# An explicit order for the opening, later pieces of w_out, and a forward SSD pass that carries its state ahead and gates a chunk behind

## The chip, the cores and the metric

The kernel runs on one core of a Trainium2 chip. The core has a matrix engine (PE), a vector engine (DVE), an activation engine (ACT) and a general engine (POOL), which issues DMAs too; SP only issues DMAs. Every engine works through its own instructions in the order in which they were laid out, and waits on semaphores of the others. The metric is the device time of one execution in microseconds (us). It was 908.02 us, the median of three runs (901.15 to 909.67).

## The reference, cut to what matters

One encoder layer on x (1024 positions, 1024 channels). A root-mean-square norm and one projection feed two groups of heads: a Mamba-2 SSD in both directions, in chunks of 128 positions, for two groups of 8 heads; and windowed attention. Each has a gate, their outputs meet in the product with w_out, and the residual and a last norm follow.

```
h = rms_norm(x, norm_in_g);  proj = h @ w_in
z, xbc, dt_raw, q, k, v, ga = split(proj);  xbc = silu(conv(xbc) + conv_b)
# SSD, per direction, chunk c:
scores = (C_c B_c^T) * exp(cs_l - cs_s)        # masked, per head
y_c    = scores @ X_c + (C_c S_c) * exp(cs_l)  # y_diag + y_off
S_c+1  = decay_c * S_c + B_c^T (decay * X_c)   # state, carried
y = y_fwd + y_bwd + d_skip * xs
y_ssd  = rms_norm_per_group(y * silu(z))
y_attn = rms_norm(windowed_gqa(q, k, v) * silu(ga))
out = rms_norm(x + concat(y_ssd, y_attn) @ w_out) * final_g
```

## The kernel before, in words

**Matrix products.** The large products split each float32 operand into a high and a low part (`hi`, `lo`) and add three products. One block of w_in (128 output channels) is 8 slices by 3 products, 24 matmuls of 512 positions for each half of the positions: `proj_steps`, line 146 before and 154 after. They are called projections below.

**Opening.** Eight tiles of x (128 positions each) are loaded, normed on ACT or DVE with POOL's power (lines 212 to 218), transposed by PE against the identity (220) and split into `hhi` on ACT and `hlo` on DVE (224, 225), in four quarters of 256 positions. Two blocks of w_in run along with the quarters.

**SSD.** For g = 0, 1: a backward pass over chunks 7 to 0, then a forward pass over 0 to 7. In the backward pass `y_off` (PE, line 570, then DVE 572) adds its part into `yb_d` in device memory by an accumulating DMA from POOL (579), and `advance` carries the state: POOL makes `xd` (542), ACT and DVE split it into `xh`, `xl` (545, 546), PE multiplies (552), POOL decays the old state (557) and DVE adds (558). In the forward pass `scores` makes M of a chunk: 8 ACT rows on E (607), a DVE addition on F (608), DVE minimum (609), ACT scaling and exponent (612, 613), three DVE products. The chunk's `yb` is y_off, to which POOL's accumulating DMA (630) adds `yb_d`; DVE adds the product with M (635, 637); POOL gates with z (`yg`, 643), ACT squares (646), POOL folds the squares (647, 649) and SP stores.

**Order.** `fill(n)` takes n halves of the projections that are still to be done. Where an instruction ends up on its engine is decided by a scheduler at build time, which estimates durations; the program's text gives only the order in which the work is named. With `tc.issue_after(x)` the text binds an instruction behind x.

**w_out.** 32 pieces (`chore`: load, two ACT copies, a POOL difference) are split during attention; `chores_up_to(32)` takes those that are left before the last products.

Of the kernel before, what the change touches and what calls it, by code (L numbers as in the profile page):

```python
# [16 lines left out]
P = 128  # L17
# [18 lines left out]
def kernel(  # L36
# [74 lines left out]
    def load_parameters():  # L111
        nc.sync.dma_start(out=prm_sb, in_=prm)
        V.tensor_scalar(out=cw, in0=cw, scalar1=0.5, scalar2=None, op0=ALU.mult)

    def rsqrt(dst, src, scale, eps):
        n = src.shape[1]
        V.tensor_scalar(out=dst, in0=src, scalar1=scale, scalar2=eps, op0=ALU.mult, op1=ALU.add)
        G.tensor_tensor(out=dst, in0=dst, in1=nhalf[:, 0:n], op=ALU.pow)
# [64 lines left out]
    both = rows(s1.tile([P, NH], F32, name="sink2"), sink, NH), rows(s1.tile([P, NH], F32, name="dsk2"), d_skip, NH)  # L183
    dtb = rows(s1.tile([P, 32], F32, name="dtb"), dt_bias, 32)
    Ab = rows(s1.tile([P, 32], F32, name="Ab"), a_log, 32)
    rb = s1.tile([64, NH], F32, name="rb")
    G.memset(rb, NEG)
    G.dma_start(out=rb[0:32], in_=rel_bias)

    dsk = gp.tile([P, NH // 2], F32, name="dsk")  # L190
    msk = gp.tile([P, 2, P], F32, name="msk")
    G.dma_start(out=msk, in_=c_tri)
    xts = [cp.tile([P, S + 4], F32, tag="pad", name="xt0")[:, 0:D]]
    xts += [tiles[3][:, 2 * i:2 * i + 2, :].rearrange("p b e -> p (b e)") for i in range(4)]
    xts += [cp.tile([P, S + 4], F32, tag="pad", name="xt5")[:, 0:D], tiles[1], tiles[0]]
    for sb, xt in enumerate(xts):
        nc.sync.dma_start(out=xt, in_=x[sb * P:(sb + 1) * P, :])
        if sb == 0:
            load_parameters()
        if sb in (1, 2):  # L200
            blk = XBC0 + 6 + 2 * sb
            pre[blk] = load_split(w_blk[blk], [P, NKB, P], wp, eng=V)
    whi, wlo = load_split(w_vdt, [P, NKB, 288], s1, tag="wv", eng=G)
    for q in range(4):
        sh, o = divmod(q, 2)
        cols = slice(o * 256, o * 256 + 256)
        banks = [bank(t) for t in ("mm t s y", "t s t s", "t s t s", "t s y t")[q].split()]
        for j, xt in enumerate(xts[2 * q:2 * q + 2]):
            junk = cp.tile([P, D], F32, tag="acc", name="junk")
            ss = s1.tile([P, 1], F32, tag="ss", name="ss", bufs=8)  # L210
            if q == j == 0:
                V.tensor_tensor_reduce(out=junk, in0=xt, in1=xt, scale=1.0, scalar=0.0, op0=ALU.mult,
                                       op1=ALU.add, accum_out=ss)
            else:
                A.activation(out=junk, in_=xt, func=AF.Square, accum_out=ss)
            rs = s1.tile([P, 1], F32, tag="rs", name="rs", bufs=8)
            rsqrt(rs, ss, 1.0 / D, EPS)
            V.tensor_scalar(out=xt, in0=xt, scalar1=rs, scalar2=None, op0=ALU.mult)
            for kb in range(NKB):
                T.transpose(banks[kb // 2][:, (kb % 2) * 256 + j * P:(kb % 2) * 256 + (j + 1) * P],  # L220
                            xt[:, kb * P:(kb + 1) * P], ident)
        for kb in range(NKB):
            ps = banks[kb // 2][:, (kb % 2) * 256:(kb % 2) * 256 + 256]
            A.activation(out=hhi[sh][:, kb, cols], in_=ps, func=AF.Copy, scale=g_in[:, kb:kb + 1])  # L224
            V.scalar_tensor_tensor(out=hlo[sh][:, kb, cols], in0=ps, scalar=g_in[:, kb:kb + 1],
                                   in1=hhi[sh][:, kb, cols].bitcast(F32),
                                   op0=ALU.mult, op1=ALU.subtract)
        for blk, ws in pre.items():
            if o == 0:
                early.setdefault(blk, []).append(bank("mm"))  # L230
            for _ in proj_steps(early[blk][sh][:, cols], ws, sh, cols):
                pass
# [248 lines left out]
    def v3(t):  # L481
        return t.rearrange("p (h d) -> p h d", h=HPG)
# [40 lines left out]
    for g in range(NG):  # L523
# [15 lines left out]

        def weighted(c, d):  # L540
            xd = sp.tile([P, 512], F32, tag="xd", name="xd")
            G.tensor_tensor(out=v3(xd), in0=v3(xk[:, c, :]), in1=bc(hb(wst, d, c, g), 64), op=ALU.mult)
            xh = sp.tile([P, 512], F32R, tag="xh", name="xh", bufs=1)
            xl = sp.tile([P, 512], F32R, tag="xl", name="xl", bufs=1)
# [4 lines left out]
        def advance(Sold, c, d):  # L549
            ps = bank("s")  # L550
            for i, (b, x) in enumerate(zip((Bk[0], Bk[0], Bk[1]), weighted(c, d))):
                T.matmul(ps, lhsT=b[:, c, :], rhs=x, start=i == 0, stop=i == 2)
            Sn = sp.tile([P, 512], F32, tag="S", name=f"S{d}")
            if Sold is None:
                A.activation(out=Sn, in_=ps, func=AF.Copy)
            else:
                G.tensor_tensor(out=v3(Sn), in0=v3(Sold), in1=bc(hb(dec, d, c, g), 64), op=ALU.mult)
                V.tensor_tensor(out=Sn, in0=Sn, in1=ps, op=ALU.add)
            return Sn
# [27 lines left out]
        def scores(c):  # L587
# [10 lines left out]
            CB = sp.tile([P, 2, P], F32, tag="CB", name="CB")  # L598
# [9 lines left out]
            V.tensor_tensor(out=F, in0=F, in1=bc(hb(ncs, 1, c, g), P), op=ALU.add)  # L608
# [11 lines left out]
        Mn = scores(0)  # L620
        for c in range(NSB):
            M = Mn
            if c < NSB - 1:
                Mn = scores(c + 1)
            yb = sp.tile([P, 512], F32, tag="yo", name="yb", bufs=3)
            if Sf is None:
                nc.sync.dma_start(out=yb, in_=yb_d[g, c])
            else:
# [11 lines left out]
            zt = sp.tile([P, 4, P], F32, tag="zt", name="zt", bufs=1)  # L640
            nc.sync.dma_start(out=zt, in_=z_d[g * 4:(g + 1) * 4, :, c * P:(c + 1) * P].rearrange("b p s -> p b s"))
            yg = sp.tile([P, 512], F32, tag="yg", name="yg", bufs=1)
            G.tensor_tensor(out=yg, in0=yb, in1=zt.rearrange("p b s -> p (b s)"), op=ALU.mult)
            nc.sync.dma_start(out=y_d[g, c], in_=yg)
            y2 = sp.tile([P, 512], F32, tag="y2", name="y2", bufs=1)
            A.activation(out=y2, in_=yg, func=AF.Square)
            G.tensor_tensor(out=y2[:, 0:256], in0=y2[:, 0:256], in1=y2[:, 256:512], op=ALU.add)
            sqs = sp.tile([P, P], F32, tag="sqs", name="sqs", bufs=6)
            G.tensor_tensor(out=sqs, in0=y2[:, 0:P], in1=y2[:, P:256], op=ALU.add)
            sums.append((g, c, sqs))  # L650
# [26 lines left out]
    def outputs():  # L677
# [51 lines left out]
        chores_up_to(32)  # L729
        for sb in range(NSB):  # L730
# [19 lines left out]
            for part in range(2):  # L750
                ys.append(parts(load_y(o_d[sb, part])))
                for dh, c0, c1 in cuts if sb < NSB - 1 else []:
                    yield from products(pss[dh], ys[part], range(8 + 4 * part, 12 + 4 * part), dh,
                                        part == 0, part == 1)
# [306 lines left out]
```

## Time and profile before

| | before |
|---|---|
| median of three runs | 908.02 us |
| the profiled execution | 900.58 us, span 898.8 us |
| PE busy | 848.2 us (94%) |
| DVE busy | 569.2 us (63%) |
| ACT busy | 491.3 us (55%) |
| POOL busy | 356.6 us (40%) |

Busy shares are means over the whole span: an engine with 40% can still be the one that is waited for in a stage of its own. Three stages are named below by their times: the opening (0 to 50 us), the backward pass of g = 1 (386.6 to 443.1 us) and its forward pass with what follows until attention starts (443.1 to 542.1 us).

### The profile page before, as it was taken

The page shows a single profiled execution, that of the slowest core. Times are in us where ns is not written, and L with a number is a line of the kernel's source. Part 1 is how long each engine was busy: PE and PEld are TensorE (multiplying, and loading weights), DVE is VectorE, ACT ScalarE, POOL GpSimd, SP SyncE. Part 2 cuts the span into 40 slices and gives each one's busy share as a digit, 9 for nine tenths or more (in the row PEclk, how much of TensorE's full clock was granted, in tenths as well). Part 3 has the DMA queues.
Part 4 walks back from the last instruction along what each step waited for, and adds up shares of the span by engine and source line. Part 5 has one row for each costly group of instructions (what it writes and reads, how often), then busy time and mean ns, then how long its engine had stood idle before and what let it go on. Part 6 is the DMA issues. An engine that isn't in the chain of part 4 may idle for free. (4 is left out here: it accounts for less than half of the span.)

```text
span 898.8 us, 13352 instructions
## 1 busy us (share of the span) xinstructions
PE 848.2 (94%) x4622; PEld 714.6 (80%) x4622; DVE 569.2 (63%) x971; ACT 491.3 (55%) x1118; POOL 356.6 (40%) x327
## 2 busy tenths in 40 slices
PE   3999999998898999999979999999999999899997
PEld 2999788886677888888857787887888888688786
DVE  4575766596898375446769945655766767555433
ACT  4642474353656345523645725788867866764222
POOL 3300012533865201134358552273653741735622
PEclk9999999999999999999998999999999999999999
DMA  8122473576788513477859869869856757424421
GB/s 296 75 83 59 155 222 128 141 222 187 223 234 256 166 47 94 117 206 177 261 131 253 225 190 246 243 200 308 245 149 182 221 131 190 145 56 136 132 87 47
DMA packets 127408, 154.25 MB, mean 172 GB/s; under 512 B 42331, under 2 KB 79899, under 8 KB 127212
## 3 DMA queue, kind: packets, MB, share of 16 engines
q1 hardware_dynamic: 121420, 141.35, 51.4%
q0 software_dynamic: 5776, 11.79, 7.4%
q8 instruction: 36, 0.59, 0.3%
q14 instruction: 32, 0.26, 0.1%
q10 hardware_dynamic: 144, 0.26, 0.1%
HBM read 111.58 MB, written 43.88 MB: 173 GB/s over the span
## 5 line engine op out<-in xcount | busy, mean ns | idle before, releaser
L146 PE MATMUL mm<-hhi,whi 128*128 128x512 f32 (+1 forms) x640 | 247.2, 389 | 1.8 <-ACT hhi L224 1.8
L146 PE MATMUL mm<-hlo,whi 128*128 128x512 f32 (+1 forms) x640 | 246.9, 387 | 0.0
L146 PE MATMUL mm<-hhi,wlo 128*128 128x512 f32 (+1 forms) x640 | 246.5, 386 | 0.0
L146 PEld LDWEIGHTS mm<-hhi,whi 128*128 128x128 f32 x640 | 121.6, 191 | 23.5 <-ACT hhi L224 2.5
L146 PEld LDWEIGHTS mm<-hlo,whi 128*128 128x128 f32 x640 | 121.9, 191 | 22.5 <-issue 1.7
L146 PEld LDWEIGHTS mm<-hhi,wlo 128*128 128x128 f32 x640 | 121.9, 191 | 21.7 <-issue 0.7
L695 PE MATMUL mm<-hhi,yl 128*128 128x512 f32 (+1 forms) x264 | 104.8, 397 | 0.8 <-POOL yl L687 0.8
L695 PE MATMUL mm<-hhi,yh 128*128 128x512 f32 (+1 forms) x264 | 104.7, 397 | 0.0
L695 PE MATMUL mm<-hlo,yh 128*128 128x512 f32 (+1 forms) x264 | 104.6, 396 | 0.0
L880 DVE CUSTOM_DVE_ANT_0 lg<-s,bias,nsnk 128x320 f32<-128x320 f32 (+2 forms) x128 | 64.6, 521 | 43.5 <-PE s L877 42.6
L883 ACT ACTIVATE lg<-lg,nm 128x320 f32<-128x320 f32 (+2 forms) x128 | 68.5, 535 | 18.3 <-DVE nm L880 16.4
L250 DVE SCALAR_TENSOR_TENSOR acc<-pad,prm_sb,acc 128x1024 f32<-128x1024 f32 x48 | 62.1, 1301 | 24.4 <-ACT acc L247 23.1
L687 POOL TENSOR_TENSOR yl<-y,yh 128x512 fp32r<-128x512 f32 x32 | 41.8, 1306 | 82.6 <-ACT yh L686 63.8
L134 ACT ACTIVATE whi<-wraw 128x1024 fp32r<-128x1024 f32 x38 | 40.0, 1054 | 41.9 <-PE mm L146 38.1
L137 POOL TENSOR_TENSOR wlo<-wraw,whi 128x1024 fp32r<-128x1024 f32 x12 | 30.2, 2518 | 69.0 <-ACT whi L134 69.0
L695 PEld LDWEIGHTS mm<-hhi,yl 128*128 128x128 f32 x264 | 50.2, 190 | 7.0 <-POOL yl L687 1.2
L607 ACT ACTIVATE cb<-cb,ncs 128x128 f32<-128x128 f32 x128 | 39.4, 390 | 29.8 <-DMA cb<-cs_d 29.8
L695 PEld LDWEIGHTS mm<-hhi,yh 128*128 128x128 f32 x264 | 50.3, 190 | 5.6
L695 PEld LDWEIGHTS mm<-hlo,yh 128*128 128x128 f32 x264 | 50.1, 190 | 5.5
L897 DVE TENSOR_TENSOR pl<-t,ph 128x512 fp32r<-128x512 f32 (+1 forms) x64 | 40.6, 654 | 18.7 <-ACT ph L896 18.0
L435 POOL TENSOR_TENSOR hlo<-oraw,hhi 128x512 fp32r<-128x512 f32 x32 | 41.0, 1292 | 26.6 <-ACT hhi L434 24.7
L137 DVE TENSOR_TENSOR wlo<-wraw,whi 128x1024 fp32r<-128x1024 f32 x26 | 33.7, 1297 | 24.0 <-ACT whi L134 21.4
(233 smaller groups left out, 1749.8 us busy)
## 6 DMA issues: line engine op xcount, KB each, us to landing
wraw<-in_w_blk_dram SPq DMA_DIRECT2D x38, 512.0 KB, 4.2
cb<-cs_d SPq DMA_DIRECT2D x32, 512.0 KB, 5.8
qt<-q_d SPq DMA_DIRECT2D x32, 256.0 KB, 3.8
oraw<-in_w_out_dram SPq DMA_DIRECT2D x32, 256.0 KB, 4.0
et<-es_d SPq DMA_DIRECT2D x56, 128.0 KB, 4.9
yb_d<-pad SPq DMA_DIRECT2D x8, 512.0 KB, 3.9
z_d<-gz SPq DMA_DIRECT2D x16, 256.0 KB, 3.8
zt<-z_d SPq DMA_DIRECT2D x16, 256.0 KB, 3.7
```

Of the source, the lines that this page charges most:

```text
L134: A.activation(out=hi, in_=raw, func=AF.Copy)
L137: eng.tensor_tensor(out=lo, in0=raw, in1=hi.bitcast(F32), op=ALU.subtract)
L146: yield T.matmul(ps, lhsT=l[:, kb, :], rhs=r[sh][:, kb, cols], start=(n == 0), stop=(n == 3 * NKB - 1))
L250: V.scalar_tensor_tensor(out=acc, in0=pad[:, k:k + S], scalar=cw[:, blk * 6 + k:blk * 6 + k + 1], in1=acc, op0=ALU.mult, op1=ALU.add)
L435: G.tensor_tensor(out=lo[:, c:c + 512], in0=raw, in1=hi[:, c:c + 512].bitcast(F32), op=ALU.subtract)
L607: A.activation(out=E[:, h, :], in_=E[:, h, :], func=AF.Identity, bias=ncs[:, 0, c, hh:hh + 1])
L687: G.tensor_tensor(out=lo, in0=t, in1=hi.bitcast(F32), op=ALU.subtract)
L695: yield T.matmul(ps[:, cols], lhsT=l[:, j * P:(j + 1) * P], rhs=r[:, dh * 512 + cols.start:dh * 512 + cols.stop], start=first and n == 0, ...
L880: V.tensor_tensor_reduce(out=l, in0=ps[:, d0 - c0:d1 - c0], in1=bias[:, hp, d0 - f0:d1 - f0], scale=-1.0, scalar=nsnk[:, sk], op0=ALU.add, ...
L883: A.activation(out=l, in_=l, func=AF.Exp, scale=-1.0, bias=nm, accum_out=sm)
L897: V.tensor_tensor(out=pl[0:w, 0:n], in0=ps[0:w, 0:n], in1=ph[0:w, 0:n].bitcast(F32), op=ALU.subtract)
```

## The change

1. **Opening.** `in_line` binds each instruction behind the one before on its engine, so norms, transposes, splits and the two early blocks stand in the order of the text. The parameters are loaded after the second x tile, the two early weight blocks after the second and fourth (they came after the second and third), and the small tables, loaded by POOL, go behind the last of POOL's norms.
2. **w_out.** The pieces are split just before the product that needs them, or one behind every third matmul of the first block; the call for all 32 is gone.
3. **Forward SSD.** The state goes ahead of the chunk's product with M, and `xd`, `xh`, `xl` of the next chunk are made ahead. The product with M is added first, and then POOL's DMA adds `yb_d`. Gating (`finish`) and folding (`reduce`) come one chunk later, and y is stored from ACT's queue. The masked CB stays in PSUM. The addition on F is now 8 ACT rows instead of one DVE instruction. `ordered` ties POOL's instructions of the SSD, its DMAs included, to one sequence, in the backward pass too.

```diff
+        def ordered(trace):
+            with ExitStack() as st:
+                if last[0] is not None:
+                    st.enter_context(tc.issue_after(last[0].ins))
+                last[0] = trace()
...
-                G.dma_start(out=yb_d[g, c], in_=yo, accum_op=ALU.add)
+                ordered(lambda: G.dma_start(out=yb_d[g, c], in_=yo, accum_op=ALU.add))
...
-            CB = sp.tile([P, 2, P], F32, tag="CB", name="CB")
+            CB = ps[:, P:3 * P].rearrange("p (d l) -> p d l", d=2)
...
-            V.tensor_tensor(out=F, in0=F, in1=bc(hb(ncs, 1, c, g), P), op=ALU.add)
+                A.activation(out=F[:, h, :], in_=F[:, h, :], func=AF.Identity, bias=ncs[:, 1, c, hh:hh + 1])
...
-        Mn = scores(0)
+        Mn, xw, ready = scores(0), weighted(0, 0), None
         for c in range(NSB):
             M = Mn
             if c < NSB - 1:
                 Mn = scores(c + 1)
             yb = sp.tile([P, 512], F32, tag="yo", name="yb", bufs=3)
-            if Sf is None:
-                nc.sync.dma_start(out=yb, in_=yb_d[g, c])
-            else:
+            first = Sf is None
+            if not first:
                 y_off(Sf, c, 0, yb)
-                G.dma_start(out=yb, in_=yb_d[g, c], accum_op=ALU.add)
+            if c < NSB - 1:
+                Sf = advance(Sf, c, 0, xw)
+            y2 = finish(*ready) if ready else None
+            if c < NSB - 2:
+                xw = weighted(c + 1, 0)
+            if y2 is not None:
+                reduce(c - 1, y2)
             fill(FORWARD[c][0])
...
-            V.tensor_tensor(out=yb, in0=py, in1=yb, op=ALU.add)
-            if c < NSB - 1:
-                Sf = advance(Sf, c, 0)
...
+            if first:
+                V.tensor_copy(yb, py)
+            else:
+                V.tensor_tensor(out=yb, in0=py, in1=yb, op=ALU.add)
+            ordered(lambda: G.dma_start(out=yb, in_=yb_d[g, c], accum_op=ALU.add))
+            ready = c, yb
...
+        reduce(NSB - 1, finish(*ready))
...
+                chores_up_to(2 * kb + 2)
...
-        chores_up_to(32)
```

PE in the forward pass of g = 1, before, from the product with the state of chunk 1 (`CT,S`; `xh`, `xl` are the operands of `advance`, `M,xk` the product with M, `mm` the projections):

```order
L570 MATMUL s<-CT,S_3950 128x128 x4
L552 MATMUL s<-xh,Bk_2737 128x512
L552 MATMUL s<-xl,Bk_2737 128x512
L552 MATMUL s<-xh,Bk_2738 128x512
L146 MATMUL mm<-hhi_100,wlo 128x512
L146 MATMUL mm<-hhi_100,whi 128x512
L146 MATMUL mm<-hlo_102,whi 128x512
```

The same place now, from the last product of the backward pass to the third of the forward pass:

```order
L154 MATMUL mm<-hhi_99,wlo 128x512
L627 MATMUL s<-CT,S_3633 128x128 x4
L713 MATMUL y<-M,xk 64x128 x8
L611 MATMUL s<-xh,Bk_2785 128x512
L611 MATMUL s<-xl,Bk_2785 128x512
L611 MATMUL s<-xh,Bk_2786 128x512
L653 MATMUL t<-CT,BT 128x128
L627 MATMUL s<-CT,S_3812 128x128 x4
```

No projection follows here until attention's first product; before, 11 to 48 stood in a chunk. Counted from the first `advance` of the group, the backward pass now holds 444 projections (193 before) and the forward pass none (266 before until attention).

POOL in the forward pass of g = 1, before:

```order
L643 TENSOR_TENSOR yg<-yb,zt 128x512
L630 DMA yb<-yb_d 128x512
L137 TENSOR_TENSOR wlo<-wraw,whi 128x1024
L557 TENSOR_TENSOR S_4198<-S_4056,dec 128x512
L647 TENSOR_TENSOR y_3958<-y_3958 128x256
L542 TENSOR_TENSOR xd<-xk,wst 128x512
```

and now, one chunk and the next DMA:

```order
L719 DMA yb<-yb_d 128x512
L608 TENSOR_TENSOR S_4103<-S_3955,dec 128x512
L681 TENSOR_TENSOR yg<-yb,zt 128x512
L598 TENSOR_TENSOR xd<-xk,wst 128x512
L688 TENSOR_TENSOR y_4114<-y_4114 128x256
L690 TENSOR_TENSOR sqs<-y_4114 128x128
L719 DMA yb<-yb_d 128x512
```

The gating of a chunk (`yg`) now stands behind its own DMA and ahead of the next chunk's DMA; before, the next DMA was issued straight behind `yg` and landed beside the work after it.

## Rows read from the trace of the kernel before

**Rows 1.** PE and the rest by stage: us, busy (x instructions), granted PE clock.

```profile
0.00:20.00 20.00, 6.18 (x25) 5.12 (x26) 7.34 (x16) 8.36 (x14) 7.61 (x26) 1.00 0.86 283
...
386.60:443.10 56.50, 56.50 (x285) 46.89 (x284) 37.71 (x46) 25.13 (x61) 22.79 (x19) 1.00 0.79 202
443.10:528.80 85.70, 75.64 (x418) 60.73 (x416) 66.77 (x77) 44.26 (x107) 51.84 (x41) 0.96 0.75 207
528.80:542.10 13.30, 13.25 (x73) 10.79 (x73) 3.81 (x6) 2.66 (x4) 6.99 (x10) 1.00 0.58 175
...
205.70:289.30 83.60, 74.19 (x427) 59.18 (x425) 68.84 (x76) 46.65 (x115) 51.74 (x41) 0.98 0.77 230
```

**Rows 2.** What PE waited for, whole span: us in total, times, longest.

```profile
PE mm L220 <- DVE xt L218: 11.9, 1, 11.9
PE y L635 <- DVE yb L637: 6.2, 3, 2.4
PE s L552 <- DVE xl L546: 5.7, 5, 2.2
...
PE t L891 <- DVE pl L897: 3.4, 1, 3.4
```

**Rows 3.** Two projections in PE's timeline, 17 starts apart (start, us).

```profile
389.37 0.39 PE L146 MATMUL mm<-hhi,whi 128*128 128x512 f32 x1
...
393.22 0.40 PE L146 MATMUL mm<-hhi,wlo 128*128 128x512 f32 x1
```

**Rows 4.** DMA issues: KB each, median us to landing; then line 630's minimum, median, maximum.

```profile
yb_d<-yo POOLq DMA_DIRECT2D x14, 256.0 KB, 5.4
yb<-yb_d POOLq DMA_DIRECT2D x14, 256.0 KB, 5.7
...
DMA to landing us min/median/max: 4.1/5.7/6.8
```

**Rows 5.** Groups of POOL instructions: busy, mean ns | idle before, releaser.

```profile
L542 POOL TENSOR_TENSOR xd<-xk,wst 128x512 f32<-128x512 f32 x28 | 31.5, 1129 | 20.8 <-DVE xl L546 17.5 <-ACT xk L265 3.3
L643 POOL TENSOR_TENSOR yg<-yb,zt 128x512 f32<-128x512 f32 x16 | 26.9, 1680 | 38.7 <-DVE yb L637 35.3 <-DMA zt<-z_d 3.2
L647 POOL TENSOR_TENSOR y<-y 128x256 f32<-128x256 f32 x16 | 19.3, 1207 | 6.1 <-ACT y L646 6.1
L649 POOL TENSOR_TENSOR sqs<-y 128x128 f32<-128x128 f32 x16 | 12.1, 755 | 0.8
```

**Rows 6.** Groups of the scores and the state, on ACT and DVE.

```profile
L607 ACT ACTIVATE cb<-cb,ncs 128x128 f32<-128x128 f32 x128 | 39.4, 390 | 29.8 <-DMA cb<-cs_d 29.8
L612 ACT ACTIVATE M<-CB,dt 128x128 f32<-128x128 f32 x128 | 38.9, 390 | 0.8 <-DVE CB L600 0.7
L608 DVE TENSOR_TENSOR cb<-cb,ncs 128x1024 f32<-128x1024 f32 x16 | 22.2, 1386 | 13.2 <-DMA cb<-cs_d 13.2
L613 ACT ACTIVATE cb<-cb 128x1024 f32<-128x1024 f32 x16 | 16.9, 1057 | 18.9 <-DVE cb L609 18.8
```

**Rows 7.** POOL in the forward pass of g = 1 (timeline).

```profile
463.21 0.72 POOL L647 TENSOR_TENSOR y<-y 128x256 f32<-128x256 f32 x1 [0.74 <-ACT y L646]
...
470.77 1.27 POOL L643 TENSOR_TENSOR yg<-yb,zt 128x512 f32<-128x512 f32 x1 [3.52 <-DVE yb L637]
471.99 0.90 POOL L630 DMA_DIRECT2D yb<-yb_d  x1
...
480.70 0.45 POOL L649 TENSOR_TENSOR sqs<-y 128x128 f32<-128x128 f32 x1
```

**Rows 8.** The opening: three rows of the timeline, then a group.

```profile
4.25 1.22 DVE L212 CUSTOM_DVE_ANT_0 junk<-xt 128x1024 f32<-128x1024 f32 x1 [4.25 <-DMA xt<-in_x_dram]
...
11.09 0.74 DVE L218 TENSOR_SCALAR xt<-xt,rs 128x1024 f32<-128x1024 f32 x1
...
50.28 0.30 PE L286 MATMUL mm<-wvhi,hhi 128*128 128x288 f32 x1
...
L225 DVE SCALAR_TENSOR_TENSOR hlo<-t,prm_sb,hhi 128x256 fp32r<-128x256 f32 x14 | 6.7, 480 | 7.4 <-ACT hhi L224 7.2
```

More of the change, by code (lines that the diff above doesn't have):

```diff
@@ L112, in load_parameters @@
         nc.sync.dma_start(out=prm_sb, in_=prm)
-        V.tensor_scalar(out=cw, in0=cw, scalar1=0.5, scalar2=None, op0=ALU.mult)
     def rsqrt(dst, src, scale, eps):
@@ L117, in rsqrt, with in_line @@
         V.tensor_scalar(out=dst, in0=src, scalar1=scale, scalar2=eps, op0=ALU.mult, op1=ALU.add)
-        G.tensor_tensor(out=dst, in0=dst, in1=nhalf[:, 0:n], op=ALU.pow)
+        return G.tensor_tensor(out=dst, in0=dst, in1=nhalf[:, 0:n], op=ALU.pow)
+    def in_line(line, trace):
+        with ExitStack() as st:
+            for ins in line.values():
+                st.enter_context(tc.issue_after(ins.ins))
+            ins = trace()
+        line[str(ins.ins.engine)] = ins
+        return ins
     pa = ctx.enter_context(ExitStack())
@@ L181, in rows, with small_tables @@
         return t
[L183 to L192, printed above, removed]
+    def small_tables():
+        both = rows(s1.tile([P, NH], F32, name="sink2"), sink, NH), rows(s1.tile([P, NH], F32, name="dsk2"), d_skip, NH)
+        dtb = rows(s1.tile([P, 32], F32, name="dtb"), dt_bias, 32)
+        Ab = rows(s1.tile([P, 32], F32, name="Ab"), a_log, 32)
+        rb = s1.tile([64, NH], F32, name="rb")
+        G.memset(rb, NEG)
+        G.dma_start(out=rb[0:32], in_=rel_bias)
+        dsk = gp.tile([P, NH // 2], F32, name="dsk")
+        msk = gp.tile([P, 2, P], F32, name="msk")
+        G.dma_start(out=msk, in_=c_tri)
+        return both, dtb, Ab, rb, dsk, msk
     xts = [cp.tile([P, S + 4], F32, tag="pad", name="xt0")[:, 0:D]]
@@ L195 @@
     xts += [cp.tile([P, S + 4], F32, tag="pad", name="xt5")[:, 0:D], tiles[1], tiles[0]]
+    raw = {}
     for sb, xt in enumerate(xts):
         nc.sync.dma_start(out=xt, in_=x[sb * P:(sb + 1) * P, :])
-        if sb == 0:
+        if sb == 1:
             load_parameters()
[L200 to L203, printed above, removed]
+        if sb in (1, 3):
+            blk = XBC0 + 7 + sb
+            raw[blk] = wp.tile([P, NKB, P], F32, tag="wraw", name="wraw", bufs=3)
+            nc.sync.dma_start(out=raw[blk], in_=w_blk[blk])
@@ new lines, with split_first, norm @@
+    line = {}
+    def split_first(blk):
+        hi = wp.tile([P, NKB, P], F32R, tag="whi", name="whi")
+        lo = wp.tile([P, NKB, P], F32R, tag="wlo", name="wlo")
+        in_line(line, lambda: A.activation(out=hi, in_=raw[blk], func=AF.Copy))
+        in_line(line, lambda: V.tensor_tensor(out=lo, in0=raw[blk], in1=hi.bitcast(F32), op=ALU.subtract))
+        pre[blk] = hi, lo
+    def norm(i):
+        xt = xts[i]
+        junk = cp.tile([P, D], F32, tag="acc", name="junk")
+        ss = s1.tile([P, 1], F32, tag="ss", name="ss", bufs=8)
+        if i in (0, 4):
+            in_line(line, lambda: V.tensor_tensor_reduce(out=junk, in0=xt, in1=xt, scale=1.0, scalar=0.0,
+                                                         op0=ALU.mult, op1=ALU.add, accum_out=ss))
+        else:
+            in_line(line, lambda: A.activation(out=junk, in_=xt, func=AF.Square, accum_out=ss))
+        rs = s1.tile([P, 1], F32, tag="rs", name="rs", bufs=8)
+        in_line(line, lambda: V.tensor_scalar(out=rs, in0=ss, scalar1=1.0 / D, scalar2=EPS, op0=ALU.mult, op1=ALU.add))
+        in_line(line, lambda: G.tensor_tensor(out=rs, in0=rs, in1=nhalf[:, 0:1], op=ALU.pow))
+        in_line(line, lambda: V.tensor_scalar(out=xt, in0=xt, scalar1=rs, scalar2=None, op0=ALU.mult))
@@ new lines, with turn @@
+    tbanks = {}
+    def turn(i):
+        q, j = divmod(i, 2)
+        if j == 0:
+            tbanks[q] = [bank(t) for t in ("mm t s y", "t s t s", "t s t s", "t s y t")[q].split()]
+        for kb in range(NKB):
+            o = (kb % 2) * 256 + j * P
+            in_line(line, lambda: T.transpose(tbanks[q][kb // 2][:, o:o + P], xts[i][:, kb * P:(kb + 1) * P], ident))
+    norm(0)
+    norm(1)
+    V.tensor_scalar(out=cw, in0=cw, scalar1=0.5, scalar2=None, op0=ALU.mult)
+    turn(0)
+    turn(1)
@@ L204 @@
+    first, second = raw
+    split_first(first)
     for q in range(4):
@@ L206 @@
         cols = slice(o * 256, o * 256 + 256)
[L207 to L213, printed above, removed]
-            else:
[L215 to L221, printed above, removed]
-        for kb in range(NKB):
[L223 to L227, printed above, removed]
+        for kb in range(NKB):
+            ps = tbanks[q][kb // 2][:, (kb % 2) * 256:(kb % 2) * 256 + 256]
+            g, h, l = g_in[:, kb:kb + 1], hhi[sh][:, kb, cols], hlo[sh][:, kb, cols]
+            in_line(line, lambda: A.activation(out=h, in_=ps, func=AF.Copy, scale=g))
+            in_line(line, lambda: V.scalar_tensor_tensor(out=l, in0=ps, scalar=g, in1=h.bitcast(F32),
+                                                         op0=ALU.mult, op1=ALU.subtract))
+            if kb % 4 == 3 and q < 3:
+                norm(2 * q + 2 + kb // 4)
+        if q == 0:
+            split_first(second)
         for blk, ws in pre.items():
@@ L230 @@
                 early.setdefault(blk, []).append(bank("mm"))
-            for _ in proj_steps(early[blk][sh][:, cols], ws, sh, cols):
-                pass
+            steps = proj_steps(early[blk][sh][:, cols], ws, sh, cols)
+            for n in range(3 * NKB):
+                in_line(line, lambda: next(steps))
+                if blk == second and q < 3 and n in (0, 12):
+                    turn(2 * q + 2 + n // 12)
+    whi, wlo = load_split(w_vdt, [P, NKB, 288], s1, tag="wv", eng=G)
+    with tc.issue_after(line["EngineType.Pool"].ins):
+        both, dtb, Ab, rb, dsk, msk = small_tables()
     for t, src in zip((snk, dsk), both):
@@ L538 @@
             kv_pools.append(pool(ctx, "kvp", side="left"))
+        last = [None]
+        def ordered(trace):
+            with ExitStack() as st:
+                if last[0] is not None:
+                    st.enter_context(tc.issue_after(last[0].ins))
+                last[0] = trace()
         def weighted(c, d):
[L541 to L544, printed above, removed]
+            xd = sp.tile([P, 512], F32, tag="xd", name="xd", bufs=1)
+            ordered(lambda: G.tensor_tensor(out=v3(xd), in0=v3(xk[:, c, :]), in1=bc(hb(wst, d, c, g), 64), op=ALU.mult))
+            xh = sp.tile([P, 512], F32R, tag="xh", name="xh")
+            xl = sp.tile([P, 512], F32R, tag="xl", name="xl")
             A.activation(out=xh, in_=xd, func=AF.Copy)
@@ L547, in weighted, with advance @@
             return xh, xl, xh
-        def advance(Sold, c, d):
+        def advance(Sold, c, d, xw=None):
+            Sn = sp.tile([P, 512], F32, tag="S", name=f"S{d}")
+            if Sold is not None:
+                ordered(lambda: G.tensor_tensor(out=v3(Sn), in0=v3(Sold), in1=bc(hb(dec, d, c, g), 64), op=ALU.mult))
             ps = bank("s")
-            for i, (b, x) in enumerate(zip((Bk[0], Bk[0], Bk[1]), weighted(c, d))):
+            for i, (b, x) in enumerate(zip((Bk[0], Bk[0], Bk[1]), xw or weighted(c, d))):
                 T.matmul(ps, lhsT=b[:, c, :], rhs=x, start=i == 0, stop=i == 2)
-            Sn = sp.tile([P, 512], F32, tag="S", name=f"S{d}")
             if Sold is None:
@@ L752, in outputs @@
                 for dh, c0, c1 in cuts if sb < NSB - 1 else []:
-                    yield from products(pss[dh], ys[part], range(8 + 4 * part, 12 + 4 * part), dh,
-                                        part == 0, part == 1)
+                    for n, m in enumerate(products(pss[dh], ys[part], range(8 + 4 * part, 12 + 4 * part), dh,
+                                                   part == 0, part == 1)):
+                        yield m
+                        if sb == part == 0 and n % 3 == 2:
+                            chore()
             for i, (dh, c0, c1) in enumerate(cuts):
```

28 lines of the change are left out of this document (15 added, 13 removed).

## The prediction, made before the changed kernel ran

> **What bounds the kernel now.** I read the busy shares first: PE works 94% of the span, so a change pays only where PE stands, and costs wherever it makes PE stand. The windows by stage show where that is. The opening leaves PE busy for 6.2 of 20 us. In g = 1 the backward pass (386.6 to 443.1 us) has PE busy through all of its 56.5 us; the forward pass and its tail (443.1 to 528.8) leave 10.1 us of 85.7 open, and the last 13.3 us before attention are full. The forward pass of g = 0 leaves 9.4 us open [rows 1]. The list of PE's waits names the causes: 11.9 us for the first normed tile, and in the SSD, at most 2.4 us at a time, 6.2 us for DVE's yb and 5.7 for its xl [rows 2]. So all that a better forward pass can win is the open part of the two stages, about 20 us, with at most 14 us in the opening; behind that is the matmul work itself.
>
> **What fills PE in the SSD.** The chain of the state is thin for PE: a chunk of the forward pass needs some 2.5 us of it. The rest are projections, one every 0.2265 us (3.85 us for 17 starts [rows 3]). Whoever spends projections early has none later. This is what the new order does: 444 stand in the backward pass of g = 1 instead of 193, and none in the forward pass. The count comes from the order, the price from the rows.
>
> **Backward pass of g = 1.** 251 projections more, at 0.2265 us, are 57 us, and PE had no idle time there to take them in [rows 1]; the pass grows from 56.5 to about 113.5 us. Tying POOL's instructions into a sequence costs nothing here: between a y_off and the `advance` behind it stand 40 to 46 projections, 9 to 10.5 us, while the six steps between (y_off's DVE row, POOL's DMA issue of 0.90 [rows 7], decay, xd of 1.13 [rows 5], the splits on ACT and DVE), none of them longer than yg's 1.68, come to at most 8.8 us. If that cover were gone, PE would stand up to 8.8 us per chunk.
>
> **Forward pass of g = 1.** With nothing to fill it, its length is that of its slowest engine's sequence. POOL's is now a closed ring per chunk: issue the DMA that adds yb_d, wait until it has landed (the decay lies within), gate (`yg`), make `xd` of the chunk after next, fold, fold again, issue the next DMA. `yg` cannot pass its own DMA and the next DMA cannot pass the folds. The landing is 5.7 us in the median, between 4.1 and 6.8 [rows 4]; yg 1.68, xd 1.13, the folds 1.21 and 0.755 [rows 5]: 10.5 us a chunk. Before, the DMA of the next chunk was issued straight behind yg, 471.99 after the yg of 470.77, and its flight lay beside the folds, xd and decay [rows 7]. Six chunks with xd at 10.5 and two without at 9.35 make 81.7 us. The ring can start only when the backward pass's last addition to yb_d has landed (5.4 us [rows 4], with a product and a DVE row ahead of it: I take 7 us after the last product). Sum: 88 us; I take 86, since the first products with M stand ready and the last wait overlaps attention's first rows. All of this replaces 85.7 + 13.3 = 99.0 us [rows 1], and 15 projections (3.4 us) are left for attention: 57 + 86 + 3.4 − 99 = **+47 us**. PE has about 20 us of work in these 86.
>
> The bounds: with the shortest landing [rows 4] and the shortest yg and folds (1.27, 0.72, 0.45 [rows 7]) a chunk takes 7.7 us and the pass 66, which gives +27. From above, ACT's work per chunk is not much shorter than the ring: L607 costs 39.4/16 = 2.46 us a chunk, and now twice (F moves over from DVE, which saves it 1.39 us there [rows 6]), L612 2.43, the exponent 1.06 [rows 6]: 8.4 us, without the copies for the state and the squares. Where both sequences wait for one another, 12.5 us a chunk are possible, 107 us in all: +68. I stay with 10.5, since the ring's members have the more direct rows.
>
> A rule stands against the landing time. The Trainium skill, "DMA: Bandwidth & Descriptors", section "Anatomy of one DMA — SWDGE (gpsimd) path", gives a fit of 2.0 us plus the bytes at 436 GB/s for a DMA from this engine, 2.6 us for 256 KB by my estimate from it; then a chunk would take 7.4 us and the pass about 61, for +22 there. The row of 5.7 us for these very DMAs disagrees, and I go by the row.
>
> **Forward pass of g = 0.** The same change, but here 132 to 158 projections remain in the forward pass by the order: 33 us, with some 20 for the chain 53. PE needs nothing of the ring's last two turns, so the pass is 88 − 19 = 69 us to it, some 4 of them taken up by the next group's first work. PE stands 12 us, where it stood 9.4 [rows 1]: +2, between −9 (all waits gone) and +8 (POOL's pads for the next group stand behind the ring and hold up its convolutions).
>
> **Opening.** PE can start on the first tile at about 7 instead of 11.9 us: DVE's scale of it stood at 11.09, behind the second tile's norm [rows 8]. Now it follows its own landing at 4.25: square 1.22, two short rows for the power, scale 0.74 [rows 8]. That is up to 4.9 us won at the start. Against it, the new order is serial from quarter to quarter: eight splits on ACT and DVE, in which the second of a bank waits for DVE's part of the first (0.48 us each [rows 8], three in a row and the hand-overs: 1.55 us per pair, 6.2 for four); two norms in the same queues, 2 us; and then PE's remaining products with the next transposes between them, 3 us. 11.2 to 11.7 us a quarter, four times, from a start at 11 to 12 us, when the second tile is transposed: the end lies at 56 to 59 us. The dt and v columns began at 50.28 [rows 8], and about 3 us of work that came behind that now lies ahead of it. I take **+6**; −3 if the quarters overlap more than the text suggests, +15 if PE, working in short stretches, stays at the lower clock throughout. The small tables behind POOL's last norm are needed late; nothing.
>
> **w_out.** The pieces stand in the orders of ACT and POOL almost where they were, up to the last ones. The one wait there that could go is 3.4 us [rows 2]. I take 0, between −4 and +1. The store from ACT's queue, CB in PSUM and the earlier state are hidden by the ring or save DVE time that nobody waits for; 0.
>
> **Sum.** 47 + 2 + 6 = +55 us on the profiled execution, 900.6 us: 955.6. That execution lay 7.4 us under the median of the runs, which spread over 8.5 us; I add 4.5 and predict **960 us**. About 9 us, 1%, is the least that a measurement of this kernel tells from no change.
>
> **The rivals.**
> - *The ring is short, and ACT or DVE sets the forward pass.* If the DMAs land faster with an idle PE and fewer loads around them, a chunk takes 7 to 8 us and the pass 60 to 68: +21 to +29 there, and with the other terms 925 to 942 us. For it: the shortest landing was 4.1 us [rows 4], and DVE had 66.8 us of work in the old stage of 85.7, which included splits of weights that are now gone [rows 1]. Against it: in the same stage the DMAs were slow with a queue as full as it will be now. Chance 0.17.
> - *Faster.* The waits for yb, xl and S go (12 us [rows 2]) because the state runs ahead, the opening wins 5 us, w_out 3, and the backward pass is not paid for, since POOL's delays there would have stalled PE and the projections only fill those stalls: 908 − 20 = 888 us. It decides at the forward pass: with a chunk under 3.5 us, PE, with 20 us of work and nothing to fill, would lose less than it did. No row comes near it: yg, xd and the folds alone are 4.8 us [rows 5]. Chance 0.07.
> - *The gains and the losses cancel.* The ring at its shortest (+27), the opening at −3, g = 0 at −9 and w_out at −4 leave +11 over the profiled run, about 912 us. Chance 0.07.
> - *The opening is the larger loss.* A cold PE in four separate stretches, +15, and 12.5 us a chunk: 985 to 990 us. Chance 0.08.
> - The forecast itself, 945 to 978 us: 0.61.
>
> **Range and chances.** 915 to 990 us takes in all but the faster case, the lower half of the cancelling one and what is unknown above: about 0.85. The likeliest case's own range is 945 to 978. Slower by over 1%: 0.87 (forecast, ring short, opening, and a little of the cancelling case). Within 1%: 0.06. Faster by over 1%: 0.07.
>
> **What the new profile would show.** Right: PE at 100% in a longer backward pass of g = 1, about 113 us between its first `advance` and its last product with the state; then some 85 us with PE at a quarter, POOL's `yg` waiting for its DMA by 4 us or more in each chunk, and `yb` DMAs some 10.5 us apart; PE's granted clock, 0.96 in the old stage [rows 1], well lower. PE's first matmul near 7 us and the first product of the dt and v columns (50.3 us before) later than 54. Wrong: `yb` DMAs 5 to 7 us apart, or a forward pass in which PE waits mostly for M (then ACT or DVE sets it), or idle PE time in the backward pass, which would mean that the projections there hid stalls and cost less than 57 us.

## The result, and the profile after

The changed kernel takes 974.75 us (median of four runs, 974.0 to 976.3), against 907.34 before (four runs; the 908.02 further up is the median of three of them): 1.0765 times as long, with a 95% interval of 1.0729 to 1.0801. The profiled execution took 976.3 us, 75.7 more than the one before. The forecast was 960, within 915 to 990.

The windows of the changed kernel by stage (as in [rows 1]: the stretch, its length, the busy time of PE, PE's weight loads, DVE, ACT and POOL with their instructions, the granted clock, DMA share, GB/s). The granted clock is a mean over the stretch: 1.00 is 2.4 GHz, 0.50 is 1.2 GHz. The cuts are landmarks of PE's order: the products with the hot rows, which end the opening (110.9), the first `advance` of g = 0 (167.6) and of g = 1 (416.8), its last product with the state in the backward pass (531.4), and the point at which attention goes on (616.0):

```profile
0.00:110.90 110.90, 96.15 (x571) 87.05 (x572) 65.26 (x114) 47.84 (x83) 17.95 (x38) 0.92 0.35 114
110.90:167.60 56.70, 55.13 (x257) 44.85 (x257) 28.93 (x27) 34.44 (x65) 6.28 (x11) 1.00 0.60 185
167.60:283.00 115.40, 115.40 (x549) 95.72 (x548) 49.88 (x64) 48.27 (x112) 25.11 (x21) 1.00 0.54 151
283.00:360.00 77.00, 66.83 (x363) 53.05 (x364) 68.74 (x68) 51.72 (x135) 47.85 (x42) 0.87 0.58 166
360.00:416.80 56.80, 49.23 (x239) 40.63 (x236) 37.54 (x33) 33.47 (x54) 12.44 (x16) 0.94 0.59 164
416.80:531.40 114.60, 114.60 (x541) 94.71 (x539) 53.73 (x64) 46.00 (x109) 24.94 (x21) 1.00 0.65 173
531.40:616.00 84.60, 44.31 (x229) 32.06 (x227) 48.69 (x59) 37.40 (x109) 48.12 (x48) 0.64 0.55 147
616.00:974.50 358.50, 340.61 (x1888) 289.08 (x1888) 205.46 (x532) 224.31 (x580) 165.56 (x133) 0.98 0.57 166
```

Read the last three rows against [rows 1]. The backward pass of g = 1 was 56.5 us and is 114.6, with PE busy throughout. The forward pass and its tail were 99.0 us and are 84.6, with PE idle for 40 of them and its granted clock at 0.64. Together 199.2 us stand where 155.5 stood: +43.7. From attention on, 358.5 us stand where 356.7 stood (898.8 − 542.1).

Ahead of these, the opening and g = 0 up to the first `advance` of g = 1, before (two rows) and after (one row, the sum of four above):

```profile
0.00:102.00 102.00, 87.40 (x570) 81.51 (x570) 60.62 (x112) 47.13 (x85) 18.02 (x38) 1.00 0.38 123
102.00:386.60 284.60, 275.19 (x1385) 225.78 (x1385) 193.34 (x198) 147.09 (x283) 93.70 (x90) 0.99 0.60 174
...
110.90:416.80 305.90, 286.59 (x1400) 234.25 (x1400) 185.08 (x190) 167.89 (x365) 91.68 (x89) 0.96 0.57 163
```

In the opening PE stands as long as before (14.75 us, before 14.6), but as many rows keep it busy for 8.75 us longer, at a lower granted clock. From 15 to 25 us that clock is 0.50, after ten microseconds (5 to 15) in which PE worked for 6.9. Part of g = 0's longer time is of this kind too.

What PE waited for in the changed kernel (us in total, times, longest), against [rows 2]:

```profile
PE t L566 <- POOL sqs L690: 19.1, 6, 7.7
PE mm L154 <- ACT pad L292: 9.1, 2, 7.6
PE s L611 <- ACT xh L601: 8.6, 5, 2.3
PE mm L247 <- DVE xt L237: 7.1, 1, 7.1
PE mm L154 <- DVE hlo L263: 5.0, 3, 2.5
PE y L713 <- DVE M L674: 4.6, 2, 4.0
PE s L611 <- DVE xl L602: 3.6, 3, 2.0
...
PE y L713 <- DVE yb L718: 2.0, 2, 1.5
...
PE y L713 <- DVE yb L716: 1.7, 1, 1.7
```

The wait for yb is down from 6.2 to 3.7 us, as the change wants. At the head stands one that came to 0.5 us before: the sums of squares (`sqs`), POOL's last rows of each turn of the ring.

POOL in the forward pass of g = 1 (start, us): the first issue, one turn with the issue that begins the next, and the end of the pass:

```profile
540.62 0.90 POOL L719 DMA_DIRECT2D yb<-yb_d  x1 [1.29 <-issue]
...
550.03 0.90 POOL L719 DMA_DIRECT2D yb<-yb_d  x1
550.65 1.37 POOL L608 TENSOR_TENSOR S<-S,dec 128x512 f32<-128x512 f32 x1
554.48 1.27 POOL L681 TENSOR_TENSOR yg<-yb,zt 128x512 f32<-128x512 f32 x1 [2.47 <-DMA yb<-yb_d]
555.71 1.04 POOL L598 TENSOR_TENSOR xd<-xk,wst 128x512 f32<-128x512 f32 x1
557.73 0.73 POOL L688 TENSOR_TENSOR y<-y 128x256 f32<-128x256 f32 x1 [0.98 <-ACT y L683]
558.54 1.31 POOL L690 TENSOR_TENSOR sqs<-y 128x128 f32<-128x128 f32 x1
559.80 0.89 POOL L719 DMA_DIRECT2D yb<-yb_d  x1
...
606.32 0.88 POOL L719 DMA_DIRECT2D yb<-yb_d  x1
611.37 1.25 POOL L681 TENSOR_TENSOR yg<-yb,zt 128x512 f32<-128x512 f32 x1 [4.17 <-DMA yb<-yb_d]
613.36 0.72 POOL L688 TENSOR_TENSOR y<-y 128x256 f32<-128x256 f32 x1 [0.74 <-ACT y L683]
614.17 0.45 POOL L690 TENSOR_TENSOR sqs<-y 128x128 f32<-128x128 f32 x1
```

Each turn is the ring that the forecast described: issue, wait for the landing, gate, xd, folds, issue. The first fold mostly waits for ACT's squares too (0.98 and 0.74 here), which the forecast had not counted. This turn took 9.77 us; the first issue stands at 540.62 and the eighth at 606.32, 9.4 us a turn on average. Line 719's landing is shorter than it was in [rows 4]:

```profile
  POOL yg L681: 49.9, 15
...
DMA to landing us min/median/max: 3.9/4.5/7.3
```

### The profile page after: what moved, and what is told of

Its sections match the earlier page's. It is cut to its first block, busy times and chain, and to the rows that moved or that the text cites. A ratio compares the mean times of both kernels' runs of the same rounds, so it can differ in the third digit from the quotient of the medians.

```text
span 974.5 us, 13449 instructions
## 1 busy us (share of the span) xinstructions
PE 882.3 (91%) x4622; PEld 737.2 (76%) x4622; DVE 558.2 (57%) x957; ACT 523.4 (54%) x1244; POOL 348.3 (36%) x329
## 5 line engine op out<-in xcount | busy, mean ns | idle before, releaser
L154 PE MATMUL mm<-hhi,whi 128*128 128x512 f32 (+1 forms) x640 | 250.3, 391 | 10.6 <-ACT pad L292 9.1
L154 PE MATMUL mm<-hlo,whi 128*128 128x512 f32 (+1 forms) x640 | 250.6, 392 | 5.5 <-DVE hlo L263 5.0
L954 DVE CUSTOM_DVE_ANT_0 lg<-s,bias,nsnk 128x320 f32<-128x320 f32 (+2 forms) x128 | 64.5, 521 | 44.4 <-PE s L951 43.7
L636 POOL DMA_DIRECT2D yb_d<-yo x14 | 12.5, 891 | 185.0 <-DVE yo L629 172.5
L297 DVE SCALAR_TENSOR_TENSOR acc<-pad,prm_sb,acc 128x1024 f32<-128x1024 f32 x48 | 69.0, 1441 | 14.6 <-ACT acc L294 13.4
L145 DVE TENSOR_TENSOR wlo<-wraw,whi 128x1024 fp32r<-128x1024 f32 x24 | 30.4, 1268 | 44.0 <-ACT whi L142 43.9
L665 ACT ACTIVATE cb<-cb,ncs 128x128 f32<-128x128 f32 x128 | 40.0, 393 | 19.3 <-DMA cb<-cs_d 19.3
```

The source lines that it names most:

```text
L145: eng.tensor_tensor(out=lo, in0=raw, in1=hi.bitcast(F32), op=ALU.subtract)
L154: yield T.matmul(ps, lhsT=l[:, kb, :], rhs=r[sh][:, kb, cols], start=(n == 0), stop=(n == 3 * NKB - 1))
L297: V.scalar_tensor_tensor(out=acc, in0=pad[:, k:k + S], scalar=cw[:, blk * 6 + k:blk * 6 + k + 1], in1=acc, op0=ALU.mult, op1=ALU.add)
L636: ordered(lambda: G.dma_start(out=yb_d[g, c], in_=yo, accum_op=ALU.add))
L665: A.activation(out=F[:, h, :], in_=F[:, h, :], func=AF.Identity, bias=ncs[:, 1, c, hh:hh + 1])
L954: V.tensor_tensor_reduce(out=l, in0=ps[:, d0 - c0:d1 - c0], in1=bias[:, hp, d0 - f0:d1 - f0], scale=-1.0, scalar=nsnk[:, sk], op0=ALU.add, ...
```

## The experiments

Each is an edit of one of the two kernels. The kernel before ran beside each group (1 to 4, 5 to 8, 9 to 12), at medians of 906.66, 904.92 and 903.87 us.

**1. POOL bound in the forward passes only** (changed kernel).

```diff
-                if last[0] is not None:
+                if last[0] is not None and bound[0]:
                     st.enter_context(tc.issue_after(last[0].ins))
...
+        last[0], bound[0] = None, True
         Mn, xw, ready = scores(0), weighted(0, 0), None
```

> The changed kernel with POOL's sequence bound in the forward passes only; in the backward passes it is free, as before. By the order, the backward pass of g = 1 then holds 160 projections up to its last two chunks (444 in the whole pass with the change) and the forward pass again some 20 a chunk. Theory (the binding made the scheduler spend the projections early, and the empty forward pass is what costs): g = 1 goes from 199 us back to 155 to 165, g = 0 gives back 10 to 15, and the time is 912 to 930 us; the POOL ring of about 9.5 us a chunk is then hidden by 20 projections (4.5 us) and the chain. Rival (the ring itself costs, whatever fills PE): the forward pass stays near 84 us with 30 us or more of PE idle, and the backward pass does not win; 945 us or more.

Measured: 914.44 us, 1.0103 times before (1.0064 to 1.0142). 60 of the 67 us are gone. g = 0, from the hot rows to the first `advance` of g = 1, takes 286.5 us in place of 305.9, and g = 1 takes 150.8 in place of 199.2:

```profile
112.70:399.20 286.50, 279.84 (x1385) 229.03 (x1385) 176.15 (x189) 167.86 (x364) 94.81 (x91) 0.98 0.61 173
399.20:550.00 150.80, 145.19 (x773) 118.26 (x772) 97.34 (x119) 83.50 (x217) 74.72 (x69) 0.98 0.79 209
```

The ring is still there, but projections fill PE beside it. The theory holds; both stages gave back more than it said (19.4 us in g = 0, and g = 1 below 155).

**2. The opening of before** in the changed kernel: loads, norms, transposes and splits in before's code, which leaves their order to the scheduler.

```diff
-        if sb in (1, 3):
-            blk = XBC0 + 7 + sb
...
+        if sb in (1, 2):
+            blk = XBC0 + 6 + 2 * sb
+            pre[blk] = load_split(w_blk[blk], [P, NKB, P], wp, eng=V)
...
-            in_line(line, lambda: A.activation(out=h, in_=ps, func=AF.Copy, scale=g))
+            A.activation(out=hhi[sh][:, kb, cols], in_=ps, func=AF.Copy, scale=g_in[:, kb:kb + 1])
```

> The changed kernel with the opening of before. Theory (the traces put 8.8 us of the loss ahead of the product with the hot rows, 102.05 before and 110.86 after): 963 to 968 us, and the empty forward pass stays as it is. Rival (the opening carries the 20 us by which the forecast was short): 945 to 955 us.

Measured: 962.49 us, 12.3 us less. The new opening costs a little more than the 8.8 us that the landmark shows; it does not carry the whole miss. The trace shows what it costs: up to the hot rows PE stands as long as with the new opening (14.2 us for 14.75), but is busy for 8.5 us less, at a granted clock of 1.00 for 0.92:

```profile
0.00:101.90 101.90, 87.66 (x570) 81.59 (x571) 60.57 (x112) 47.22 (x85) 19.06 (x38) 1.00 0.37 124
```

**3. The ring without its landing** (changed kernel).

```diff
+            yl = sp.tile([P, 512], F32, tag="yl", name="yl")
+            nc.sync.dma_start(out=yl, in_=yb_d[g, c])
...
-            ordered(lambda: G.dma_start(out=yb, in_=yb_d[g, c], accum_op=ALU.add))
+            V.tensor_tensor(out=yb, in0=yb, in1=yl, op=ALU.add)
```

> The changed kernel with one step of the ring taken out: yb_d comes by a plain load from SP into a tile of its own and DVE adds it (0.7 to 1 us more per chunk on DVE), so POOL's gating no longer waits for an accumulating DMA that can start only when the sum is made. The projections stay early. Theory (POOL's ring with the landing sets the empty forward pass): 4 to 4.5 us a chunk go, g = 1's forward pass falls from 84 to 55 to 65 us, g = 0 wins up to 8: 940 to 955 us. Rival (ACT, with 8.4 us or more a chunk, or DVE sets it): 965 to 975 us.

Measured: 961.5 us, 13 less: between the two. The empty forward pass fell from 84.6 to about 70.5 us, less far than expected:

```profile
527.50:598.00 70.50, 41.90 (x227) 31.85 (x227) 55.48 (x63) 37.06 (x107) 45.72 (x39) 0.66 0.60 174
...
537.00:587.00 50.00, 30.25 (x160) 23.01 (x160) 47.71 (x54) 32.11 (x95) 35.75 (x29) 0.64 0.58 179
```

DVE is now busy for 55 of 70 us, and for 47.7 of the 50 from 537 to 587. So the landing did set the pass, and DVE, to which the edit gives eight additions more, sets it 14 us below; the 55 to 65 us were too low. DVE was not far off in the changed kernel either: 26.9 of 30 us from 560 to 590.

**4. The new opening alone** on the kernel before: the second experiment's diff the other way round.

> The kernel before with the new opening alone. Theory: 8 to 10 us slower than before, 915 to 918 us. Rival (the loss in the opening is hidden later, where PE is waiting for the convolutions anyway): within 3 us of before.

Measured: 907.70 us, 1.0022 times before (0.9994 to 1.0050). My theory failed here. The trace shows why only in part. The products with the hot rows stand at 111.8 us (102.05 before), so the opening does lose 9.8 us there, again with PE busy for longer (96.8 us for 87.4) at a lower granted clock (0.91). But the order further on differs as well, and g = 1 runs faster:

```profile
398.20:549.70 151.50, 143.41 (x775) 117.94 (x775) 113.19 (x128) 72.78 (x170) 86.09 (x69) 0.99 0.80 211
```

That is 151.5 us for 155.5, 4 us back. This execution took 909.67 us, and the one of before that is compared with it, 900.58, was among the fastest of its kind; what the opening is worth in the medians stays open between 1 us (on the old SSD) and 12 us (on the new one).

**5. The binding alone** on the kernel before: accumulating DMA, decay and xd of the backward passes tied into one sequence, with the decay named ahead of xd as in the changed kernel.

```diff
-                G.dma_start(out=yb_d[g, c], in_=yo, accum_op=ALU.add)
+                ordered(lambda: G.dma_start(out=yb_d[g, c], in_=yo, accum_op=ALU.add))
...
+                ordered(lambda: G.tensor_tensor(out=v3(Sn), in0=v3(Sold), in1=bc(hb(dec, d, c, g), 64), op=ALU.mult), d == 1)
```

> The kernel before with one thing of the change: POOL's instructions of the backward passes (accumulating DMA, decay, xd) bound into one sequence. By the order, this alone puts 38 to 51 projections between the product with the state and the next advance in each chunk of both backward passes, and leaves none in the forward pass of g = 1 behind its first chunk. Theory (early projections make the loss): 935 to 950 us, with the forward pass of g = 1 mostly without work for PE. Rival (the new forward pass with its ring is needed for the loss): within 1% of before, 900 to 915 us.

Measured: 949.37 us, 1.0506 times before (1.0472 to 1.0540). One idea of the change, with the old opening and the old forward pass, makes most of the loss. Its trace has the same shape: g = 0 longer (301.7 us from the hot rows to the first `advance` of g = 1, before 284.6), then in g = 1 a full stretch up to the last projection, at 523, and an empty one until attention goes on:

```profile
101.80:403.50 301.70, 282.48 (x1399) 230.36 (x1399) 205.54 (x200) 147.75 (x285) 94.39 (x88) 0.97 0.58 165
403.50:523.10 119.60, 117.56 (x557) 96.52 (x556) 64.52 (x72) 41.99 (x88) 30.61 (x27) 1.00 0.67 170
523.10:587.90 64.80, 36.41 (x214) 28.56 (x212) 48.68 (x57) 30.44 (x81) 47.03 (x42) 0.66 0.71 188
```

**6. Experiments 1 and 2 together**: bound in the forward passes only, opening of before.

> The changed kernel with POOL bound in the forward passes only, and with the opening of before. Theory (the two losses are separate and add up): the 12 us that the old opening gave in the second run go off the first run's 914.4, which makes 900 to 905 us, a little faster than before. Rival (with PE full again, the opening is hidden or the order changes for other reasons, as the new opening alone cost nothing against before): 908 to 915 us.

Measured: 902.07 us, 0.9981 times before (0.9954 to 1.0007). The two losses add up: 12.4 us below the first run, 10.6 if each is taken against the kernel before of its own group. It is not told apart from before.

**7. The w_out rule alone** on the kernel before.

```diff
+                chores_up_to(2 * kb + 2)
...
-        chores_up_to(32)
...
+                        if sb == part == 0 and n % 3 == 2:
+                            chore()
```

> The kernel before with the new w_out rule alone. On every engine its order is, row for row, that of before, so the theory is no difference beyond the spread of before itself (899 to 909 us), and the run is a second trace of the order of before: the place where it differs from the first trace shows where that spread comes from. Rival (the moved text changes something that the order doesn't show): outside of 899 to 909 us.

Measured: 904.53 us, 1.0014 times before (0.9988 to 1.0040). No difference, as the unchanged order of the engines' rows had it. Its trace has a span of 901.8 us and g = 1 at 156.4. Where the spread of before (899 to 910 us) comes from it does not show.

**8. No binding at all, opening of before** (changed kernel).

```diff
-                if last[0] is not None:
+                if False:
                     st.enter_context(tc.issue_after(last[0].ins))
```

> The changed kernel with no binding of POOL at all and the opening of before; the state still runs ahead of the product with M, and gating comes a chunk behind. Theory (the binding is the loss, the rest of the new forward pass is at best a small gain): 900 to 906 us. Rival (the scheduler needs the binding in the forward pass, else POOL's gating comes late and holds up the state): 910 us or more.

Measured: 906.51 us, 1.0022 times before (0.9993 to 1.0050): just outside the theory's range, and short of the rival's. Against the sixth run the binding in the forward passes is worth 4.4 us by the medians, with intervals against before that overlap (0.9954 to 1.0007 there).

**9. Pads written by DVE** (changed kernel).

```diff
-        G.memset(pad[:, 0:2], 0.0)
-        G.memset(pad[:, S + 2:S + 4], 0.0)
+        V.memset(pad[:, 0:2], 0.0)
+        V.memset(pad[:, S + 2:S + 4], 0.0)
```

> The changed kernel with one edit: the zero columns of the convolutions' pads (0.1 us each) are written by DVE, not by POOL, where they stand behind the ring of g = 0. PE's order stays the same. Theory (in g = 0 the loss that the forecast missed is these pads behind the ring: PE waited 9.1 us for pad, 7.6 in one piece): 7 to 9 us less, 965 to 968 us, and the wait for pad is gone from the list. Rival (PE waits for the ring's sums or for DVE there in any case): 972 to 976 us.

Measured: 972.17 us (969.76 to 975.19), 2.6 less than the changed kernel (974.0 to 976.3), and the runs overlap. The wait became shorter and others took its place:

```profile
PE t L566 <- POOL sqs L690: 19.0, 7, 7.4
...
PE s L611 <- ACT xh L601: 7.6, 6, 2.3
PE mm L154 <- ACT pad L292: 5.0, 1, 5.0
```

The theory falls: the pads are at most a small part of what g = 0 lost.

**10 to 12. On the sixth run's kernel**: F on DVE again (10), yb_d loaded by SP with the third experiment's diff (11), both (12).

```diff
-                A.activation(out=F[:, h, :], in_=F[:, h, :], func=AF.Identity, bias=ncs[:, 1, c, hh:hh + 1])
+            V.tensor_tensor(out=F, in0=F, in1=bc(hb(ncs, 1, c, g), P), op=ALU.add)
```

> The sixth run's kernel (bound in the forward passes, old opening) with the addition on F back on DVE. Theory (there PE waits 10.1 us for xh, which stands on ACT behind 16 rows of scores a chunk): the wait for xh shrinks to 3 to 5 us, 896 to 900 us. Rival (DVE, with 1.4 us more a chunk, then holds up xl, S or yb by as much): 901 to 906 us.

Measured: 904.71 us, 1.0019 times before (0.9995 to 1.0043). The wait for xh fell from 10.1 to 5.1 us, and one for DVE's S rose from 2.4 to 7.0. The rival holds.

> The sixth run's kernel with yb_d loaded by SP and added on DVE, which takes the accumulating DMA out of the ring. Theory (with projections to fill PE the ring is hidden, so its landing is worth little): within 3 us of the sixth run, 899 to 905 us. Rival (the ring still sets the forward passes, where PE stands about 17 us in all): 4 to 8 us faster, 894 to 898 us.

Measured: **889.92 us**, 0.9859 times before (0.9823 to 0.9894): the fastest kernel of the study, faster than both. Its two SSD stages, from the first `advance` of g = 0 to that of g = 1 and from there to attention:

```profile
155.50:382.90 227.40, 220.55 (x1132) 181.53 (x1131) 153.51 (x168) 132.05 (x298) 84.13 (x72) 0.99 0.60 171
382.90:531.10 148.20, 143.38 (x774) 117.92 (x773) 103.79 (x129) 83.08 (x217) 74.35 (x63) 0.99 0.80 216
```

The sixth run's took 233.2 and 150.4 us. So the ring's landing had still cost time in the filled forward passes, and the rival was right, with more than it claimed (12 us by the medians of two groups, 8.7 between the two traces). The tenth and twelfth runs, which differ by the same edit within one group, say the same: 11.9 us by the medians. By which path the landing held PE up stays open: neither run's list of waits names the ring, and the wait that shrank is the one for ACT's xh (10.1 to 6.9 us).

> Both edits of the two runs before it on the sixth run's kernel: F on DVE and yb_d loaded by SP. Theory (what is left of PE's idle time in the forward passes is waits for ACT's xh and for the ring together): 892 to 898 us, faster than before by 1%. Rival (PE's idle time moves to DVE's rows, which grow by 2 us a chunk): 900 to 906 us.

Measured: 892.83 us, 0.9889 times before (0.9853 to 0.9924): within the theory's range, but not better than the eleventh. The gain comes with that edit alone; with the landing gone, F is no worse on ACT than on DVE.

## Why the prediction was right, and where it was off

- **The backward pass of g = 1, 113.5 us**: 114.6, with PE busy through all of it. The price of 251 projections more, and that nothing was idle there to take them, held.
- **The forward pass, 86 us**: 84.6. Sizes were off and nearly cancelled, which is luck. The ring starts 9.2 us after the last product (531.40 to 540.62), not 7. A turn takes 9.4 us, not 10.5: the landing is 4.5 us in the median, not 5.7, and most turns wait for ACT's squares besides. The pass ends with the sums of squares, for which PE waits through the last two turns nearly whole (7.1 and 7.7 us), where I let attention cover a part. Experiment 3 shows that the landing sets this pass and that DVE comes 14 us behind.
- **Two signs of that pass failed**: `yg` waited for its DMA by 2.0 to 4.3 us, by 4 or more in only two of eight turns, since the decay fills the start of the flight. And PE was busy for 44.3 us, half of the time, not 20 and a quarter: a row of sixteen products with M took 1.09 us at 545.4 and 1.98 at 564.3, in a stretch of granted clock 0.50.
- **The Trainium skill's fit**, "DMA: Bandwidth & Descriptors", section "Anatomy of one DMA — SWDGE (gpsimd) path", would have 2.6 us for this DMA by my estimate. No landing of line 719 was under 3.9 us.
- **The cause**: the forecast had it that early projections leave the forward pass empty. Experiments 1 and 5 show it from both sides: without the binding in the backward passes 60 us return, and the binding alone costs 44.5. No run keeps the binding and gives the projections back; but PE was busy through the whole bound pass, so nothing else of the binding shows there.
- **The forward pass of g = 0, +2, at most +8**: this step failed. From the hot rows' products to the first `advance` of g = 1 it is 305.9 us (110.9 to 416.8) for 284.6 (102.0 to 386.6), +21.3. Three parts make it up. PE stands 19.3 us there (1.6, 10.2 and 7.6 in the rows above) for 9.4: +9.9. It works 15 projections more, 3.4 us: these are the ones that the forecast left for attention. And the other 1385 rows, as many as before, took 8.0 us longer, with the granted clock at 0.96 in place of 0.99 (0.87 and 0.94 in the last two stretches); the forecast had counted that at nothing. The cause is that of g = 1: experiment 1 brings the stage back to 286.5 us, and the binding alone makes it 301.7. I had counted the projections of this pass as one sum of work beside the ring, and let the next group's first work cover its last two turns. In the trace 106 of them stand from 283 to 316 us, and then almost none for three turns of the ring. First all of PE there, then its projections alone:

```profile
316.00:346.40 30.40, 20.60 (x113) 15.16 (x113) 27.02 (x28) 20.03 (x63) 19.00 (x21) 0.66 0.74 215
...
316.00:346.40 30.40, 2.11 (x8) 1.43 (x8) 0.66 0.74 215
```

- **What PE waited for in g = 0**: xh, xl, the sums and the convolution's pads in turn, as it takes its rows in order. Experiment 9 shows that the pads by themselves are not the cause; the other waits were not tried one by one.
- **The opening, +6**: 8.8 us at the landmark, 12 by experiment 2, within the bounds, but not by the mechanism that I took +6 for. PE starts at 7.1 us as forecast, and the serial order behind it costs about what that wins: PE's idle time up to the hot rows is that of before. What is lost is the clock, 8.75 us of longer rows, which stood in the forecast only as its outer bound; no row of before shows the +15 there. So the size is luck. One sign was wrong: the first dt and v products do not come later than 54 us but at 50.4; only the bulk of them waits, until 61.5.
- **w_out, 0**: right on the kernel before, by experiment 7.
- **The sum**: 47 + 2 + 6 = 55 against 75.7 between the traces: 43.7 for g = 1, 1.8 from attention on, 21.3 for g = 0 and 8.9 for the opening (by the cuts). So 19 of the 21 us between forecast and trace are g = 0's. The medians moved by 67.4. In the list of rivals, 925 as the lower end of the short ring does not come out of its terms: 900.6 + 4.5 + 21 + 8 is 934. Nothing else rests on it.

## What to carry to other kernels

An edit that binds a sequence on one engine can move the work of another: here POOL was bound and PE's filler moved. Before running such an edit, count the filler between landmarks of the busiest engine's order, stage by stage; a stage that is left with none is priced by its slowest ring. Compare PE's busy time for the same rows as well as its idle time: in the opening and in g = 0, 17 us went into longer rows at a lower granted clock, and idle time alone does not show them. Where a ring holds a DMA that can start only when its sum is ready, a plain load ahead of time and an addition take the landing out of it.

## What was not expected of the hardware

DVE's and POOL's rows of one size have two lengths. In the forward pass of g = 1 of the changed kernel, DVE's last product for M took 2.29 us beside POOL's decay, and 1.21 us later with POOL waiting:

```profile
541.39 2.29 DVE L674 TENSOR_TENSOR M<-M,cb 128x1024 f32<-128x1024 f32 x1
...
562.79 1.21 DVE L674 TENSOR_TENSOR M<-M,cb 128x1024 f32<-128x1024 f32 x1
```

POOL's decay ran from 541.23 to 542.60, over the first 1.21 us of the longer row; from 561.84 to 564.01 POOL had nothing to do. The Trainium skill, "GPSIMD Engine Reference", section "Specifications", says that the two engines share their access to SBUF where DVE has two operands there; the rows agree. No run separates the two. The accumulating DMA landed in 4.5 us in the median instead of 5.7, in g = 0 (4.6), where projections still filled part of the pass, as in g = 1 (4.4). The DMA share of these stages was lower too (0.58 and 0.55, before 0.77 and 0.75); what shortens the landing was not tried.
